# A conditioned two-layer decoder trunk: groups of three experts last in each layer, modulation loaded in pairs of vectors

## The chip, the cores and the metric

The kernel runs on one core of a Trainium2 chip. The metric is the device time in microseconds, median of the runs; lower is better. Engines are called as in the profile: PE is TensorE (PEld its weight loads), DVE is VectorE, ACT is ScalarE, POOL is GpSimd, SP is SyncE, which here only issues transfers.

## The reference, cut to what matters

One sequence of 256 rows of 1024 numbers (float32) goes through two layers and a final normalisation. `c` is a vector of 1024 that conditions every layer.

```python
for layer in range(2):
    shift_m, scale_m, gate_m, shift_f, scale_f, gate_f = split(silu(c) @ ada_w[layer] + ada_b[layer], 6)
    h = rmsnorm(x, norm_mix[layer]) * (1 + scale_m) + shift_m
    x = x + gate_m * (even_mixer if layer == 0 else odd_mixer)(h)
    h = rmsnorm(x, norm_ffn[layer]) * (1 + scale_f) + shift_f
    x = x + gate_f * grouped_moe(h)          # 16 experts, two per token
return rmsnorm(x, final_norm)
```

`ada_w[layer]` is 1024 x 6144 (25 MB), so the six modulation vectors of a layer cost 12 pieces of 2 MB. An expert has three matrices of 1024 x 512 (gate, up) and 512 x 1024 (down), 2 MB each; all 16 are read in both layers (201 MB of the 291 MB in all). The even mixer is sparse and block attention with a position bias, the odd one latent and sliding-window attention.

## The kernel before, in words

**Slots.** All weights go through a ring of tiles of 1 MB (128 partitions x 2048 float32): 10 of the pool `ring` (tag "w", `slot` in the trace) and 5 of the pool `rooms` (tag "wx", `room`). `slot()` takes the next one in the order that the list `order` gives; `left()` sets that order ahead of an MoE so that all 15 are used in turn. In the mixers the rooms hold attention data (`carve`). A load waits until the products that read the slot before are done. SP issues nearly all loads in program order.

**Modulation.** `fills` lists the pieces of 512 columns still to do, as (layer, n). `ada_load` loads one in two transfers (rows of 512 columns, 2 KB packets); `ada_chunk` multiplies it by silu(c): eight products of 32 x 512 (L332), four of them side by side in the four column groups of the array. The first half of a vector is copied out (L342), the second added (L344), and `ada_end` brings the vector into its place: eight small products for shift and scale (L307 to L313), or two products and two adds into the broadcast `GATE` (L301, L303). Four pieces are done at the start, ten within the even mixer by `ada_steps` (a piece every 9 ticks and a few more, between the mixer's own instructions), two at the MoE's start (`fill(12)`, with lowered priority); in layer 1 two at the start, four within, two at the MoE's start. ADC holds ada_b by feature, NRM the norms' gains.

**Bias rows.** `bias_line` writes the position bias of 8 heads to `scr` in DRAM; `bias_rows` (L407) reads it back by POOL's queue as 128 shifted rows, 1 MB.

**Experts.** `moe` routes each token to two experts. Experts 14 and 15 make the first group, whose weights need no routing. The other 14 are sorted by their count of tokens; `RANKS` gives the rank for each place, and `GROUPS` the places of each group with the number of blocks of 32 rows that each gets. Every group has four blocks (128 rows), so one tile of TensorE's output holds a group. Per group: `gather` (L1066), gate and up products (`hidden`, L1084, tiles `mm` and `sc`), a transpose, down products (`rows`, L1084, tile `o`) and `combine` (L1144, L1145). The loop runs gate and up of group i, then the down products of group i-1. Within a weight the slots come half by half, all experts of the group side by side.

**Overflow.** Ahead of group 3 stands `rest()`: nested branches (L1453) for tokens that found no place, on PE, ACT, DVE and SP. It allocates six slots. Group 2's down weights are loaded ahead of it, group 3's weights by POOL's queue:

```python
            if i == 3:
                before.load_down()
                flush()
                rest()
```

**The end.** In layer 1 the last group's down weights come in three column pieces (512, 256 and 256), with the final normalisation behind each (`Final`, `finish`).

Of the kernel before, what the change touches and what calls it, by code (L numbers as in the profile page):

```python
# [107 lines left out]
def trunk(ctx, tc, ins, out):  # L108
# [141 lines left out]
    def ada_load(layer, n):  # L250
        return load_k8(ins["ada_w"][layer][:, n * 512:(n + 1) * 512])

    first = [ada_load(0, n) for n in range(2)]
# [8 lines left out]
    first += [ada_load(0, n) for n in range(2, 4)]  # L262
    csil = cp.tile([P, 8, 33], F32, name="csil")
    vec.memset(csil, 0.0)
    act.activation(csil[:, :, 1], cT, AF.Silu)

    HALF = cp.tile([P, 2], F32, name="HALF")
    vec.tensor_reduce(HALF, ident.rearrange("p (g r) -> p r g", r=32)[:, 0:2], AX.X, ALU.add)
# [26 lines left out]
    def ada_end(layer, v, t):  # L295


        if v in (2, 5):
            for half in range(2):
                b = bank("tp", [P, 512])  # L300
                mm(b, HALF[:, half:half + 1].to_broadcast([P, P]), t, start=True, stop=True)  # L301
                sl = slice(half * 512, half * 512 + 512)
                vec.tensor_tensor(GATE[v][:, sl], GATE[v][:, sl], b, ALU.add)  # L303
            return
        b = bank("tp", [64, 8, 2])
        for k in range(8):
            mm(b[:, k, :], t[:, 64 * k:64 * k + 64], HALF, start=True, stop=True)  # L307
        o = MOD[layer, v]
        for half in range(2):
            sl = slice(64 * half, 64 * half + 64)  # L310
            vec.tensor_tensor(o[sl], b[:, :, half], ADC[sl, layer, v, :], ALU.add)
        if v in (1, 4):
            vec.scalar_tensor_tensor(o, o, 1.0, NRM[:, (v // 3) * 2 + layer, :], ALU.add, ALU.mult)  # L313
# [4 lines left out]
    fills = []  # L318

    halves = []  # L320

    def ada_chunk(layer, c, W):


        v, half = divmod(c, 2)
        if half == 0 and v in (2, 5):
            GATE[v] = big.tile([P, D], F32, name="GATE", tag="GATE")
            pool.dma_start(GATE[v], ins["ada_b"][layer:layer + 1, v * D:(v + 1) * D].to_broadcast([P, D]))
        b = bank("tp", [P, 512])
        for k in range(8):  # L330
            g = (k % 4) * 32
            mm(b[g:g + 32], csil[:, k, 1 - half:33 - half], W[k], start=k < 4, stop=k >= 4)  # L332
            if k == 3:
                yield
        if half == 0:
            halves.append(ada_tile())
        t = halves[0]
        o, i = t, b
        if v not in (2, 5):
            o, i = t.rearrange("p (k m) -> p m k", k=8), b.rearrange("p (m k) -> p m k", k=8)  # L340
        if half == 0:
            act.copy(o, i)  # L342
            return
        vec.tensor_tensor(o, o, i, ALU.add)  # L344
        yield
        ada_end(layer, v, halves.pop())

    def fill(n=1):
        for _ in range(n):
            if fills:  # L350
                layer, c = fills.pop(0)
                W = first.pop(0) if first else ada_load(layer, c)
                for _ in ada_chunk(layer, c, W):
                    pass

    def ada_steps(n, rest):
# [4 lines left out]
        for i, at in enumerate(todo):  # L361
# [3 lines left out]
            yield from ada_chunk(*at, W)  # L365
# [37 lines left out]
    def bias_rows(pool_):  # L403
# [3 lines left out]
        pool.dma_start(BM, bass.AP(scr.tensor, 0, [[1, P], [384, 8], [1, 256]]))  # L407
# [1370 lines left out]
```

## Time and profile before

| | |
|---|---|
| median of 3 runs | 868.94 us (868.36 to 869.42) |
| the profiled execution | 869.42 us, span 867.2 us |
| busy: PE, PEld, DVE, ACT, POOL | 746.6, 381.9, 377.8, 237.4, 115.6 us |
| mean granted TensorE clock | 0.932 of 2.4 GHz |
| transfers | 291.14 MB, mean 336 GB/s |

The span is from the first to the last instruction of the profiled execution. Layer 0's mixer runs to about 205 us, its router to 232, its experts to 472, layer 1's mixer to 596, its router to 618, its experts and the end to 867.

### The profile page before, as it was taken

What the parts mean: (1) busy time and instruction counts of PE and PEld (TensorE: products, weight loads), DVE (VectorE), ACT (ScalarE), POOL (GpSimd) and SP (SyncE); (2) the same over time, 40 slices, a digit from 0 to 9 for tenths busy, and PEclk for the clock granted to TensorE, in tenths of its full rate; (3) what the DMA queues carried; (4) which work ended last, traced back from release to release, by engine and by line L of the source; (5) the groups of instructions that cost most, each with busy time, mean ns of one, the idle gap of its engine ahead of it and who ended that gap; (6) DMA issues with size and microseconds to landing.
All of it is one profiled execution on the core that took longest, in us unless ns stands there. A gap on an engine that the chain in (4) does not pass through costs nothing. (4 is left out here: it accounts for less than half of the span.)

```text
span 867.2 us, 12251 instructions
## 1 busy us (share of the span) xinstructions
PE 746.6 (86%) x4499; PEld 381.9 (44%) x4499; DVE 377.8 (44%) x1091; ACT 237.4 (27%) x569; POOL 115.6 (13%) x118
## 2 busy tenths in 40 slices
PE   4699999999799969759997899979899967769996
PEld 1298765557443332214332568556443322214233
DVE  2285777767831231103206654876912031103214
ACT  1254545545311010001112454545111010002012
POOL 2020111233100001000011223344000001000001
PEclk9699999999699999879999999988699988979998
DMA  9999878796299998999999997733499989999992
GB/s 328 349 328 387 321 248 217 280 376 219 96 422 418 419 417 337 419 420 419 419 415 389 360 350 196 288 130 122 179 419 419 419 361 395 420 420 419 416 396 77
DMA packets 84840, 291.14 MB, mean 336 GB/s; under 512 B 9174, under 2 KB 23202, under 8 KB 63010
## 3 DMA queue, kind: packets, MB, share of 16 engines
q1 hardware_dynamic: 76976, 258.36, 77.9%
q0 software_dynamic: 4608, 29.37, 8.3%
q10 hardware_dynamic: 3186, 2.51, 0.9%
q8 instruction: 39, 0.64, 0.3%
q14 instruction: 31, 0.25, 0.1%
HBM read 289.16 MB, written 1.06 MB: 335 GB/s over the span
## 5 line engine op out<-in xcount | busy, mean ns | idle before, releaser
L1084 PE MATMUL o<-slot,hT 128*32 128x512 f32 (+2 forms) x448 | 93.5, 619 | 14.0 <-PEq L1453 13.1
L1084 PE MATMUL sc<-slot,XG 128*64 128x512 f32 (+1 forms) x416 | 92.1, 646 | 13.6 <-DMA slot<-in_moe_w_up_dram 13.6
L1111 DVE TENSOR_TENSOR hq<-sc,hid 128x512 f32<-128x512 f32 x14 | 14.7, 1049 | 184.3 <-PE sc L1084 184.3
L1084 PE MATMUL mm<-slot,XG 128*32 128x512 f32 (+1 forms) x416 | 85.9, 624 | 5.2 <-DMA slot<-in_moe_w_gate_dram 5.2
L507 ACT CAST hl<-slot 128x512 fp32r<-128x512 f32 (+2 forms) x112 | 60.7, 557 | 72.8 <-PE mm L524 45.8
L464 POOL TENSOR_TENSOR hl<-slot,hl 128x512 fp32r<-128x512 f32 x40 | 53.2, 1333 | 163.1 <-ACT hl L507 135.7
L1084 PE MATMUL mm<-room,XG 128*64 128x512 f32 (+1 forms) x224 | 57.1, 629 | 5.6 <-DMA room<-in_moe_w_gate_dram 5.6
L1084 PE MATMUL o<-room,hT 128*32 128x512 f32 (+2 forms) x208 | 58.6, 603 | 2.0 <-DMA room<-in_moe_w_down_dram 2.0
L1155 DVE SCALAR_TENSOR_TENSOR adac<-o,w,GATE 128x512 f32<-128x512 f32 (+1 forms) x29 | 21.2, 732 | 82.5 <-PE o L1084 81.5
L522 PE MATMUL mm<-HH,hl 128*128 128x256 f32 x176 | 54.5, 311 | 2.3 <-ACT HH L496 2.3
L1084 PEld LDWEIGHTS sc<-slot,XG 128*64 128x64 f32 (+1 forms) x416 | 25.3, 132 | 70.1 <-issue 48.6
L1137 ACT CAST yg<-adac 128x512 fp32r<-128x512 f32 (+1 forms) x28 | 17.1, 612 | 140.0 <-DVE adac L1155 140.0
L332 PE MATMUL tp<-slot,csil 128*32 128x512 f32 x344 | 49.2, 648 | 4.4 <-DMA slot<-in_ada_w_dram 4.2
L1084 PE MATMUL sc<-room,XG 128*32 128x512 f32 (+1 forms) x224 | 45.0, 656 | 8.3 <-DMA room<-in_moe_w_up_dram 8.3
L1068 ACT ACTIVATE XG<-tp,mod,mod 128x256 f32<-128x256 f32 (+1 forms) x32 | 17.2, 538 | 124.0 <-PE tp L1066 124.0
L524 PE MATMUL mm<-HH,hl 128*128 128x256 f32 x176 | 50.0, 286 | 0.6 <-DVE hl L464 0.6
L523 PE MATMUL mm<-HH,hl 128*128 128x256 f32 x176 | 50.4, 287 | 0.1
L1084 PEld LDWEIGHTS o<-slot,hT 128*32 128x32 f32 (+1 forms) x448 | 25.5, 125 | 54.3 <-issue 36.0
L464 DVE TENSOR_TENSOR hl<-slot,hl 128x512 fp32r<-128x512 f32 (+2 forms) x72 | 42.6, 611 | 15.3 <-ACT hl L507 15.0
L1066 PE MATMUL tp<-pick,XH 128*128 128x256 f32 (+1 forms) x128 | 41.9, 347 | 4.0 <-DVE XG L1070 2.6
L1145 DVE TENSOR_TENSOR X<-X,tp 128x512 f32<-128x512 f32 (+1 forms) x56 | 36.0, 675 | 16.5 <-PE tp L1144 16.2
L1144 PE MATMUL tp<-yg,OT 128*128 128x512 f32 (+1 forms) x112 | 36.6, 431 | 7.5 <-ACT yg L1137 3.5
(377 smaller groups left out, 1305.9 us busy)
## 6 DMA issues: line engine op xcount, KB each, us to landing
slot<-in_ada_w_dram SPq DMA_DIRECT2D x43, 1024.0 KB, 10.3
slot<-in_moe_w_gate_dram SPq DMA_DIRECT2D x37, 1024.0 KB, 15.1
slot<-in_moe_w_down_dram SPq DMA_DIRECT2D x35, 1024.0 KB, 19.7
slot<-in_moe_w_up_dram SPq DMA_DIRECT2D x34, 1024.0 KB, 18.6
room<-in_moe_w_up_dram SPq DMA_DIRECT2D x20, 1024.0 KB, 16.8
room<-in_moe_w_gate_dram SPq DMA_DIRECT2D x19, 1024.0 KB, 15.2
room<-in_moe_w_down_dram SPq DMA_DIRECT2D x17, 1024.0 KB, 18.8
slot<-in_ev_w_in_dram SPq DMA_DIRECT2D x8, 1024.0 KB, 9.5
```

The costliest lines, as they stand in the source:

```text
L332: mm(b[g:g + 32], csil[:, k, 1 - half:33 - half], W[k], start=k < 4, stop=k >= 4)
L464: eng.tensor_tensor(lo, v, hi.bitcast(F32), ALU.subtract)
L507: act.copy(hi, src)
L522: mm(o, a[0], b[0], start=start, stop=False, skip_group_check=True)
L523: mm(o, a[0], b[1], start=False, stop=False, skip_group_check=True)
L524: mm(o, a[1], b[0], start=False, stop=stop, skip_group_check=True)
L1066: mm(b, xk[i][:, t, k, :], o[:, t, 0:n], start=t == i == 0, stop=t == i == 1)
L1068: act.activation(XG[:, k, :], b, AF.Identity, bias=sh[:, k:k + 1], scale=fa[:, k:k + 1])
L1084: last[0] = mm(*args, **kw)
L1144: mm(cb, OT[:, t, :], x, start=i == 0, stop=i == 1)
L1145: vec.tensor_tensor(X[:, t, sl], X[:, t, sl], cb, ALU.add)
L1155: vec.scalar_tensor_tensor(v, y, w, gate[:, sl], ALU.mult, ALU.mult)
```

## The change

- **Order of groups.** Before, groups 2 and 4 have three experts; after, groups 5 and 6, the last two. The blocks that each rank gets are the same.
- **Modulation by two vectors at a time.** The vectors are paired as (0, 1), (2, 5) and (3, 4). `ada_load` loads 256 rows of both vectors (a part, (layer, n, j)), two transfers of 1 MB, each with 8 KB per partition (for the gates, 2 and 5, twice 4 KB). `ada_part` multiplies a part with eight products and adds four parts up (one copy, three adds). The small transposing products serve both vectors of a pair at once. Nothing of this is left at the MoE's start but `second_gate`, which spreads the sums of vector 5 (`GT5`) into `GATE`.
- **Steps.** `ada_steps` takes 12 parts in the even mixer, 6 in the odd one, each with 7 ticks of rest.
- **Bias rows.** In layer 0 the read of `scr` is issued after the last subtraction of `modulated`.
- The last group's down pieces are laid out for three experts.

```diff
-GROUPS = [[(14, 2), (15, 2)], [(0, 3), (1, 1)], [(2, 2), (3, 1), (4, 1)], [(5, 2), (6, 2)], [(7, 2), (8, 1), (9, 1)],
-          [(10, 2), (11, 2)], [(12, 2), (13, 2)]]
-RANKS = 0, 9, 1, 10, 11, 2, 3, 4, 12, 13, 5, 6, 7, 8
+GROUPS = [[(14, 2), (15, 2)], [(0, 3), (1, 1)], [(2, 2), (3, 2)], [(4, 2), (5, 2)], [(6, 2), (7, 2)],
+          [(8, 2), (9, 1), (10, 1)], [(11, 2), (12, 1), (13, 1)]]
+RANKS = 0, 9, 1, 2, 3, 4, 5, 6, 7, 10, 11, 8, 12, 13
...
-    def ada_load(layer, n):
-        return load_k8(ins["ada_w"][layer][:, n * 512:(n + 1) * 512])
+    TWOS = [(0, 1), (2, 5), (3, 4)]
+
+    def ada_load(layer, n, j):
+        v = ins["ada_w"][layer].rearrange("(p k) f -> p k f", k=8)
+        a, b = (x * D for x in TWOS[n])
+        out = []
+        for k in range(2 * j, 2 * j + 2):
+            t = slot(4, 512)
+            if b == a + D:
+                sp.dma_start(t.rearrange("p a b -> p (a b)"), v[:, k, a:a + 2 * D])
+            else:
+                sp.dma_start(t.rearrange("p (v a) b -> p v (a b)", v=2),
+                             v[:, k, :].rearrange("p (v f) -> p v f", f=D)[:, TWOS[n][0]::TWOS[n][1] - TWOS[n][0], :])
+            out.append(t)
+        return out
...
+    def second_gate(layer):
+        gate_start(layer, 5)
+        gate_end(5, 2, GT5)
...
+    def ada_part(layer, n, j, W):
+        gates = 2 in TWOS[n]
+        if j == 0:
+            if gates:
+                gate_start(layer, 2)
+            sums.append(GT5 if gates else ada_tile())
+        t = sums[0]
         b = bank("tp", [P, 512])
+        for k in range(2):
+            for g in range(4):
+                mm(b[32 * g:32 * g + 32], csil[:, 2 * j + k, :], W[k][:, g, :], start=k == 0, stop=k == 1)
...
+        if j == 0:
             act.copy(o, i)
+        else:
+            vec.tensor_tensor(o, o, i, ALU.add)
+        if j == 3:
+            yield
+            ada_end(layer, n, sums.pop())
...
-    def bias_rows(pool_):
+    def bias_rows(pool_, after=None):
         BM, = carve((8, 256))
-        pool.dma_start(BM, bass.AP(scr.tensor, 0, [[1, P], [384, 8], [1, 256]]))
+        with tc.issue_after(after.ins) if after else nullcontext():
+            pool.dma_start(BM, bass.AP(scr.tensor, 0, [[1, P], [384, 8], [1, 256]]))
...
         with tc.high_priority(-60):
-            fill(12)
+            second_gate(layer)
...
-            ada.add(ada_steps(10, 9))
+            ada.add(ada_steps(12, 7))
...
-    ada.add(ada_steps(4, 9))
+    ada.add(ada_steps(6, 7))
```

## Rows read from the trace of the kernel before

**Rows 1.** The page, rate of all transfers in 40 equal slices of the span.

```profile
GB/s 328 349 328 387 321 248 217 280 376 219 96 422 418 419 417 337 419 420 419 419 415 389 360 350 196 288 130 122 179 419 419 419 361 395 420 420 419 416 396 77
```

**Rows 2.** Chosen stretches: us, busy PE, PEld, DVE, ACT, POOL, clock, DMA share, GB/s.

```profile
45.00:205.00 160.00, 157.43 (x1108) 111.75 (x1108) 116.43 (x382) 84.55 (x230) 32.75 (x26) 1.00 0.88 303
326.50:331.50 5.00, 5.00 (x40) 1.49 (x36) 0.00 (x0) 0.00 (x0) 1.59 (x3) 0.74 0.33 87
618.00:704.00 86.00, 81.42 (x544) 34.39 (x543) 28.78 (x89) 12.74 (x24) 1.69 (x3) 0.95 1.00 412
618.00:712.50 94.50, 83.71 (x556) 35.06 (x559) 30.23 (x92) 12.74 (x24) 1.69 (x3) 0.93 1.00 410
712.50:717.00 4.50, 4.50 (x36) 1.34 (x32) 0.00 (x0) 0.00 (x0) 1.44 (x3) 0.75 0.31 76
717.00:836.00 119.00, 98.45 (x532) 33.55 (x524) 22.44 (x40) 12.39 (x22) 3.34 (x7) 0.93 1.01 418
836.00:847.00 11.00, 9.66 (x43) 3.27 (x43) 3.38 (x5) 1.82 (x4) 0.00 (x0) 1.00 1.05 363
847.00:867.20 20.20, 12.51 (x67) 6.19 (x66) 9.69 (x21) 5.92 (x18) 3.89 (x4) 0.86 0.16 60
```

**Rows 3.** Timeline of SP's queue and of POOL at layer 1's branch.

```profile
686.77 0.33 SPq L1171 DMA_DIRECT2D room<-in_moe_w_down_dram  x1
715.19 1.30 SPq L1171 DMA_DIRECT2D room<-in_moe_w_gate_dram  x2
...
690.70 0.62 POOL L1171 DMA_DIRECT2D slot<-in_moe_w_gate_dram  x1 [82.67 <-PE o L1084]
...
697.41 0.53 POOL L1171 DMA_DIRECT2D room<-in_moe_w_gate_dram  x1 [0.20 <-issue]
715.09 0.53 POOL L1171 DMA_DIRECT2D room<-in_moe_w_gate_dram  x1 [17.14 <-SPq L1453]
```

**Rows 4.** Timeline of PE: group 2's gate (second half), group 1's down, after the branch.

```profile
675.33 3.62 PE L1084 MATMUL mm<-slot,XG 128*32 128x512 f32 x32
...
686.70 3.64 PE L1084 MATMUL o<-slot,hT 128*32 128x512 f32 x32 [0.88 <-DMA slot<-in_moe_w_down_dram]
...
710.22 1.06 PE L1084 MATMUL o<-slot,hT 128*32 128x512 f32 x2 [6.23 <-PEq L1453]
```

**Rows 5.** Timeline of DVE at the end: the last group's last piece.

```profile
857.84 0.48 DVE L1155 SCALAR_TENSOR_TENSOR adac<-o,w,GATE 128x256 f32<-128x256 f32 x1 [0.51 <-PE o L1084]
```

**Rows 6.** Timeline of PE, DVE and POOL at the start, up to the modulated rows.

```profile
34.47 1.94 PE L332 MATMUL tp<-slot,csil 128*32 128x512 f32 x8 [0.72 <-DMA slot<-in_ada_w_dram]
...
29.34 0.33 DVE L311 TENSOR_TENSOR mod<-tp,ADC 64x8 f32<-64x8 f32 x2 [3.92 <-DMA ADC<-in_ada_b_dram]
...
39.51 0.33 DVE L311 TENSOR_TENSOR mod<-tp,ADC 64x8 f32<-64x8 f32 x2 [1.96 <-PE tp L307]
...
46.61 2.90 POOL L464 TENSOR_TENSOR HH<-hv,HH 128x512 fp32r<-128x512 f32 x1 [2.29 <-ACT HH L496]
```

**Rows 7.** Transfers issued in the first 30 us: size, us to landing.

```profile
room<-scr POOLq DMA_DIRECT2D x1, 1024.0 KB, 11.1
...
ADC<-in_ada_b_dram ACTq DMA_DIRECT2D x1, 48.0 KB, 22.8
```

**Rows 8.** The softmax's line that reads the bias rows: ns, first and last start.

```profile
L569 DVE CUSTOM_DVE_ANT_0 St<-sc,room x72: 277/354/426, 92.5 to 574.7; 128x128 f32<-128x128 f32 x36, 128x256 f32<-128x256 f32 x36
```

**Rows 9.** Modulation's lines L332 (two stretches), L307 and L303, busy us there.

```profile
45.00:205.00 160.00, 20.48 (x160) 4.20 (x160) 1.00 0.88 303
484.00:596.00 112.00, 8.11 (x64) 1.46 (x64) 0.94 0.73 256
...
45.00:205.00 160.00, 4.32 (x64) 4.03 (x64) 1.00 0.88 303
...
472.00:484.00 12.00, 1.37 (x2) 1.00 1.09 335
```

**Rows 10.** Timeline of DVE in layer 0's router, behind the position sums.

```profile
226.61 0.19 DVE L1042 SCALAR_TENSOR_TENSOR route<-sc,M 128x32 f32<-128x32 f32 x1 [0.85 <-PE sc L1360]
```

More of the change, by code (lines that the diff above doesn't have):

```diff
@@ L248, in trunk @@
     act.dma_start(OH, ins["k_onehot"])
-    def ada_load(layer, n):
-        return load_k8(ins["ada_w"][layer][:, n * 512:(n + 1) * 512])
-    first = [ada_load(0, n) for n in range(2)]
+    TWOS = [(0, 1), (2, 5), (3, 4)]
[12 more added lines that the diff above has]
+        return out
+    first = [ada_load(0, 0, j) for j in range(4)]
     load_const(0, cp)
@@ L261, in trunk @@
     act.dma_start(ADC.rearrange("p l v k -> p (l v) k"), ins["ada_b"].rearrange("l (v p k) -> p (l v) k", p=P, k=8))
-    first += [ada_load(0, n) for n in range(2, 4)]
-    csil = cp.tile([P, 8, 33], F32, name="csil")
+    csil = cp.tile([P, 8, 32], F32, name="csil")
     vec.memset(csil, 0.0)
-    act.activation(csil[:, :, 1], cT, AF.Silu)
-    HALF = cp.tile([P, 2], F32, name="HALF")
-    vec.tensor_reduce(HALF, ident.rearrange("p (g r) -> p r g", r=32)[:, 0:2], AX.X, ALU.add)
+    act.activation(csil[:, :, 0], cT, AF.Silu)
     ONES = cp.tile([P, P], F32, name="ONES")
@@ L293, in trunk, with gate_end, gate_start, ada_end @@
     GATE = {}
-    def ada_end(layer, v, t):
-        if v in (2, 5):
-            for half in range(2):
[L300 to L313, printed above, removed]
+    def gate_end(v, g, t):
+        for half in range(2):
+            b = bank("tp", [P, 512])
+            r = 32 * (g + half)
+            mm(b, ident[:, r:r + 1].to_broadcast([P, P]), t, start=True, stop=True)
+            sl = slice(half * 512, half * 512 + 512)
+            vec.tensor_tensor(GATE[v][:, sl], GATE[v][:, sl], b, ALU.add)
+    def gate_start(layer, v):
+        GATE[v] = big.tile([P, D], F32, name="GATE", tag="GATE")
+        pool.dma_start(GATE[v], ins["ada_b"][layer:layer + 1, v * D:(v + 1) * D].to_broadcast([P, D]))
+    def second_gate(layer):
+        gate_start(layer, 5)
+        gate_end(5, 2, GT5)
+    def ada_end(layer, n, t):
+        if 2 in TWOS[n]:
+            gate_end(2, 0, t)
+            return
+        b = bank("tp", [64, 8, 4])
+        for k in range(8):
+            mm(b[:, k, :], t[:, 64 * k:64 * k + 64], ident[:, 0:128:32], start=True, stop=True)
+        for i, v in enumerate(TWOS[n]):
+            o = MOD[layer, v]
+            for half in range(2):
+                sl = slice(64 * half, 64 * half + 64)
+                vec.tensor_tensor(o[sl], b[:, :, 2 * i + half], ADC[sl, layer, v, :], ALU.add)
+            if i:
+                vec.scalar_tensor_tensor(o, o, 1.0, NRM[:, (v // 3) * 2 + layer, :], ALU.add, ALU.mult)
     def ada_tile():
@@ L318, in trunk @@
     fills = []
[L320 to L328, printed above, removed]
+    GT5 = cp.tile([P, 512], F32, name="GT5")
+    sums = []
+    def ada_part(layer, n, j, W):
[5 more added lines that the diff above has]
+        t = sums[0]
         b = bank("tp", [P, 512])
[L330 to L333, printed above, removed]
+        for k in range(2):
+            for g in range(4):
+                mm(b[32 * g:32 * g + 32], csil[:, 2 * j + k, :], W[k][:, g, :], start=k == 0, stop=k == 1)
+            if k == 0:
                 yield
-        if half == 0:
-            halves.append(ada_tile())
-        t = halves[0]
         o, i = t, b
-        if v not in (2, 5):
+        if not gates:
             o, i = t.rearrange("p (k m) -> p m k", k=8), b.rearrange("p (m k) -> p m k", k=8)
-        if half == 0:
+        if j == 0:
             act.copy(o, i)
[L343 to L346, printed above, removed]
+        else:
[3 more added lines that the diff above has]
+            ada_end(layer, n, sums.pop())
     def fill(n=1):
@@ L350, in fill @@
             if fills:
-                layer, c = fills.pop(0)
-                W = first.pop(0) if first else ada_load(layer, c)
-                for _ in ada_chunk(layer, c, W):
+                at = fills.pop(0)
+                W = first.pop(0) if first else ada_load(*at)
+                for _ in ada_part(*at, W):
                     pass
@@ L1261, in load_down @@
                     n = sl.stop - sl.start
-                    if n == 512:
-                        tiles = [slot(4, n) for _ in range(2)]
-                    else:
-                        tile_ = slot(8, n)
-                        tiles = [tile_[:, 0:4], tile_[:, 4:8]]
+                    tiles = []
+                    while len(tiles) < len(src):
+                        tile_ = slot(2048 // n, n)
+                        tiles += [tile_[:, j:j + 4] for j in range(0, 2048 // n, 4)]
                     for k in range(0, 4, step):
```

20 lines of the change are left out of this document (9 added, 11 removed).

## The prediction

> **What bounds the kernel now.** I read the page's slices first, for the rate of the transfers along the run [rows 1]. The slices show three kinds of stretch: the first five at 321 to 387 GB/s, the two mixture-of-experts (MoE) stages at about 420, and the ends of the two mixers far below. The reader is to see that a transfer saved is worth something only in the first and second kind.
>
> The busy times of chosen stretches say which engine goes with it [rows 2]. From 45 to 205 us TensorE is busy 157.4 of 160 us while the transfers run at 303 GB/s: the even mixer is bound by TensorE. In layer 1's MoE the transfers run at 410 to 418 GB/s from 618 to 836 us with one gap, 712.5 to 717, and a slower end, 836 to 847 (363 GB/s). Then 20.2 us follow in which nothing is loaded. Layer 0 has the same gap, 326.5 to 331.5. So an MoE stage costs its 96 tiles of 1.05 MB (2.5 us each at 418 GB/s), plus the gap, plus what is left to compute after the last byte.
>
> The queues show where the gap comes from [rows 3]. At group 3 the overflow branch (L1453) stands in the program. SP issues its last tile of group 2 at 686.77 and its next at 715.19, so it is 28.4 us in the branch. GpSimd's queue carries group 3 meanwhile: three tiles by 697.41, the fourth only at 715.09, released by SP's leaving. TensorE stands 6.23 us in the branch and leaves at 710.22 [rows 4].
>
> **The order of groups, at the branch.** The ring has 15 slots (10 and 5), and `rest()` holds 6 of them. In the code's order the tiles after the first group are: gate, up of 1; down of 0; gate, up of 2; down of 1; down of 2; the 6 held; group 3. With three experts in group 2 that is 4+4+4+6+6+4+6 = 34, and 15 - 6 - 6 = 3 of group 3 find a slot before the branch is left: 37 tiles. 410 GB/s over 94.5 us is 38.7 MB, which is those 37 [rows 2]. With two experts in group 2 it is 28, and 15 - 6 - 4 = 5 of group 3: 33 tiles. The cover falls by four tiles, 10.0 us, so the queues run dry at 702.5.
>
> When do they start again? TensorE's work before the branch is the same: a group has four blocks of 32 rows either way, and TensorE is busy 81.4 of 86 us from 618 to 704 [rows 2], so it is the bound there; it loses only a wait of 0.88 us for a down tile that now comes sooner [rows 4]. It leaves at 709.3. SP's last tile waits for group 2's first gate tiles, consumed by 675.33 [rows 4]; 28.4 us later, at 703.9, SP is out, before TensorE. From the release to bytes flowing took 1.9 us (715.09 to 717). So bytes flow at 711.2: a gap of 8.7 us where it was 4.5, **+4.2 us in layer 1**. Layer 0 has the same sequence and a gap of 5.0: **+4.2** there too, since its last down tiles end the stage. Bounds for each: 0, if TensorE comes through the branch 4 us sooner; +9, if the first slot is freed only by group 2's down products after the branch, some 5 us later.
>
> **The order of groups, at the end.** Now the last group has two experts (30 us of transfers); TensorE follows the transfers by so much that it still works for 11 us after the last byte. With 45 us of transfers for the same TensorE work in each of the last two groups, TensorE waits for bytes. What is left after the last of them is half of the last 256-column piece and the chain that follows it: the last row scaling starts at 857.84 and the span ends at 867.2, 9.4 us [rows 5]; I add 2.0 for the products of the last half piece and the wait for their landing, which is 11.4 in place of 20.2: **-8.8**. Bounds: 0 (TensorE at 1.2 GHz falls behind again) and -10. The last group's down weights come in pieces of 1 and 2 KB packets; one expert more is 2.1 MB at 363 instead of 418 GB/s [rows 2]: **+0.8**.
>
> **Modulation at the start.** The last weights of scale and shift land at 34.47, and the vectors are ready from 39.51 on; a wait for the bias vectors ADC ends at 29.34 [rows 6]. Eight loads of 1.05 MB are 8.39 MB. In the fourth slice, where packets of 2 KB go, the rate is 387 GB/s [rows 1]; 8 KB packets go at 418 in the MoE [rows 2]: 1.7 us less. The bias rows' 1 MB, 11.1 us under way here [rows 7], leaves this stretch: 2.7 us less at 387 GB/s. It is covered later: the last modulated piece ends at 49.51 [rows 6], and the bias rows' first reader in the softmax starts at 92.5 [rows 8]. Together 4.4 us, if ADC keeps its time. ADC is 48 KB and needed 22.8 us [rows 7], among neighbours of 2 KB. With neighbours of 8 KB it can come later; at the worst it eats the whole gain. I take **-3.5**, bounds -6 (a lighter queue lets X and ADC come sooner too) and 0.
>
> The Trainium skill (DMA: Bandwidth & Descriptors, Specifications) gives 512 B as the least transfer for line rate. By it the larger packets would bring nothing and the sum below would be 1.7 us higher. The slices disagree, 387 against 418, and I go by them.
>
> **Modulation in the mixers.** A unit of 2 MB costs TensorE 20.48 / 10 = 2.05 us in the even mixer and 8.11 / 4 in the odd one; the four transposing ends between 45 and 205 us cost 4.32 [rows 9]. Two units per layer move from the MoE's start into the mixer, since both gates are now summed together. Even mixer: +4.1 for two units, and two ends instead of four, -2.2: **+1.9** on the engine that binds it. Bounds 0 and +5 (four adds more on VectorE, 1 us each). Odd mixer: +4.1 and one end less, -1.1, make 3.0, of which half falls in idle time of TensorE (I have no row that says which half; bounds 0 and 3.0): +1.5. The gate's two adds leave the stretch just ahead of it, 1.37 us of VectorE [rows 9]: -1.4. Sum **+0.1**.
>
> The 4 MB per layer that leave the MoE's start bring no transfer time: the queues stand nearly idle there (96 GB/s in the eleventh slice) [rows 1], as the experts aren't known yet. What goes is work among the router's: in layer 0 VectorE waits 0.85 us for a product that stands behind the gate's [rows 10]: **-0.9** (bounds 0 and -3 over both layers). The gate's bias load, two broadcasts and adds stay; their data is ready sooner.
>
> **Sum.** Start -3.5, even mixer +1.9, router -0.9, layer 0's gap +4.2, odd mixer +0.1, layer 1's gap +4.2, small packets +0.8, tail -8.8: -2.0. The profiled execution took 869.42 us (span 867.2 and 2.2 around it), so 867.4; the median of the runs is 0.5 lower, so **866.9 us**.
>
> **Rivals.** *A later restart (slower).* The first slots after the branch come with group 2's down products, not with TensorE's leaving. Place: GpSimd's sixth tile of group 3. Price 5 us in each layer: 876.9. It decides from 1 us later per layer on. For it: a ring slot is reused in turn. Against: in the trace the fourth tile was released by SP's leaving [rows 3]. Chance 0.12.
>
> *The tail stays (slower).* TensorE, idle between arrivals, drops to 1.2 GHz and comes as late as before: +8.8, 875.7. For it: the mean clock is 0.93 from 717 to 836, where one group of three experts lies [rows 2]. Against: even there it kept pace. Chance 0.10.
>
> *ADC late (no change).* The gain at the start goes: 870.4. For it: ADC's 22.8 us [rows 7]. Chance 0.20. The Trainium skill (DMA: Bandwidth & Descriptors, Queues, rings and completion order) says that an engine goes round its queues packet by packet, which would make longer neighbours delay such a load; no row shows this with 8 KB neighbours.
>
> *The gap doesn't grow (faster).* TensorE or the walk through the branch is earlier by as much as the cover is shorter: -8.4, 858.5. Against: TensorE's 81.4 of 86 us. Chance 0.13.
>
> **Numbers.** My forecast has the remaining 0.45, with its own range of 863 to 871. Some 0.2% (1.7 us) is about what a measurement here can tell from no change. Faster: 0.6 of the forecast, the last rival, a little of ADC's: 0.44. Slower: the first two rivals, a tenth of the forecast and a quarter of ADC's: 0.31. Same: 0.25. The range reaches from the last rival to the tail that stays: 858 to 876.
>
> **What would show it.** Right: transfers dry for 8 to 9 us after the first 33 tiles in each layer, SP back before TensorE; 11 to 12 us from the last byte to the end; vectors of scale ready at about 36; TensorE as full as before from 42 to 205. Wrong: a gap of under 5 or over 13 us, a tail near 20, or ADC as the last wait ahead of the scale.

## The result and the profile after

The changed kernel takes **872.67 us** (median of 8 runs, 871.32 to 876.65), the kernel before, run beside it, 867.6 (8 runs): ratio **1.0065**, 95% interval 1.0047 to 1.0083. It is slower by 5 us; the forecast was 866.9, 2.0 under the median of before as then known. The profiled execution took 871.63 us, with a span of 870.0 (before 867.2).

I put marks at the same instructions of both traces: the even mixer's first projection (L522 before, L548 after), the first transposing product of layer 0's router (L982, L1008), the product that counts the routed tokens (tile M), layer 0's last down product, the count in layer 1, and the end. The stages between them:

| stage | before, us | after, us | difference | forecast |
|---|---|---|---|---|
| start | 41.77 | 36.56 | -5.2 | -3.5 |
| even mixer | 167.60 | 174.13 | +6.5 | +1.9 |
| router of layer 0 | 16.93 | 16.48 | -0.5 | -0.9 |
| experts of layer 0 | 241.10 | 243.90 | +2.8 | +4.2 |
| odd mixer, router of layer 1 | 145.09 | 144.99 | -0.1 | +0.1 |
| experts of layer 1 and the end | 254.71 | 253.94 | -0.8 | -3.8 (+4.2 +0.8 -8.8) |
| span | 867.20 | 870.00 | +2.8 | -2.0 |

Two stages miss: the even mixer by 4.6 us, the last one by 3.0. The start was better than forecast. The stages are those of one execution of each kernel. The medians stand 5.1 us apart because the traced execution of before lies 1.8 above its median and that of after 1.0 below (2.2 + 1.8 + 1.0); what varies between executions, e15 shows.

**The start.** PE, DVE and POOL, as in [rows 6]:

```profile
28.61 1.06 PE L359 MATMUL tp<-slot,csil 128*32 128x512 f32 x8 [1.48 <-DMA slot<-in_ada_w_dram]
30.81 1.87 PE L331 MATMUL tp<-K,adac 128*64 128x4 f32 x16 [1.14 <-DVE adac L368]
36.56 0.80 PE L548 MATMUL mm<-HH,hl 128*128 128x256 f32 x2 [3.88 <-ACT HH L522]
...
32.72 0.68 DVE L336 TENSOR_TENSOR mod<-tp,ADC 64x8 f32<-64x8 f32 x4 [1.96 <-PE tp L331]
...
44.10 0.96 POOL L433 DMA_DIRECT2D room<-scr  x1
```

The last weights land 5.9 us sooner than in [rows 6] and the vectors are there at 32.72 in place of 39.51. The prediction had them ready at about 36. The add that reads ADC waits for TensorE: ADC is not the last wait. The transfers run faster there; two stretches of before, then the same of after:

```profile
10.00:20.00 10.00, 5.29 (x22) 2.63 (x15) 4.27 (x9) 2.82 (x6) 2.59 (x3) 1.00 1.07 371
20.00:30.00 10.00, 7.32 (x60) 2.88 (x58) 1.33 (x3) 1.07 (x1) 0.00 (x0) 0.93 1.07 356
```

```profile
10.00:20.00 10.00, 6.70 (x30) 3.03 (x26) 4.39 (x10) 2.82 (x6) 1.09 (x2) 0.85 1.02 396
20.00:30.00 10.00, 6.60 (x54) 1.31 (x46) 2.37 (x3) 1.06 (x1) 0.00 (x0) 0.98 1.03 392
```

**The even mixer**, as stretches in the columns of [rows 2], first the whole mixer of the kernel before, then of the one after:

```profile
41.77:209.37 167.60, 164.97 (x1136) 118.02 (x1137) 122.55 (x393) 90.07 (x240) 34.22 (x27) 0.99 0.88 305
```

```profile
36.56:210.69 174.13, 168.10 (x1137) 116.77 (x1137) 127.67 (x396) 87.37 (x237) 35.23 (x28) 0.99 0.84 306
...
195.00:200.00 5.00, 2.64 (x12) 1.54 (x12) 5.00 (x9) 2.92 (x6) 3.60 (x3) 1.00 0.01 2
200.00:210.00 10.00, 9.85 (x46) 7.21 (x46) 7.21 (x13) 4.72 (x9) 1.29 (x1) 1.00 0.01 2
```

TensorE has 3.1 us more work and 3.4 us more idle time (6.0 against 2.6). The largest piece of the idle time is a hole of 2.4 us from 195 to 200, where VectorE is full. PE's longest waits in the changed kernel's mixer:

```profile
107.33 0.65 PE L650 MATMUL o<-PT,room 128*64 128x256 f32 x4 [1.53 <-DVE PT L225]
...
197.56 0.63 PE L643 MATMUL tp<-K,St 128*128 128x128 f32 x4 [0.89 <-DVE St L633]
199.76 0.49 PE L549 MATMUL mm<-hl,o 128*128 128x512 f32 x1 [1.33 <-DVE hl L490]
```

VectorE ends each of them. In the kernel before, no wait within the mixer is over 0.71 us.

**The branches.** Stretches of layer 0 and layer 1, then SP, POOL and PE in layer 1, as in [rows 2 to 4]:

```profile
304.00:324.50 20.50, 14.35 (x87) 6.49 (x81) 8.12 (x19) 3.88 (x7) 3.47 (x7) 0.91 0.69 255
690.00:712.50 22.50, 16.20 (x104) 7.34 (x106) 8.42 (x20) 3.88 (x7) 2.82 (x6) 0.94 0.76 283
```

```profile
711.29 10.23 SPq L1197 DMA_DIRECT2D slot<-in_moe_w_gate_dram  x4
...
687.68 0.62 POOL L1197 DMA_DIRECT2D slot<-in_moe_w_gate_dram  x1 [76.56 <-DMA slot<-in_moe_w_down_dram]
694.81 1.21 POOL L1197 DMA_DIRECT2D slot<-in_moe_w_gate_dram  x2 [6.52 <-PE o L1110]
701.47 0.53 POOL L1197 DMA_DIRECT2D room<-in_moe_w_gate_dram  x1 [5.45 <-PE o L1110]
702.15 0.53 POOL L1197 DMA_DIRECT2D room<-in_moe_w_up_dram  x1 [0.15 <-issue]
711.56 0.53 POOL L1197 DMA_DIRECT2D room<-in_moe_w_up_dram  x1 [8.88 <-PEq L1478]
...
711.47 1.09 PE L1110 MATMUL o<-slot,hT 128*64 128x512 f32 x1 [4.02 <-PEq L1478]
```

Against a steady 419 GB/s the first stretch loses 20.5 x (1 - 255/419) = 8.0 us, the second 7.3. The same sum for the two stretches of [rows 2] gives 4.0 and 3.7. So each branch costs 3.6 to 4.0 us more, as forecast. The form is another than forecast: the queues run short from 304 and from 694 on, and live on slots that TensorE's down products free one by one. The count of slots held: five tiles of group 3 are issued ahead of TensorE's leaving, which releases the sixth at 711.56. SP's next load had by then waited 13.1 us for TensorE, so SP was back first, as forecast.

**The end.** Stretches, PE and DVE in the last 24 us, as in [rows 2, 5]:

```profile
846.00:854.00 8.00, 6.11 (x35) 2.18 (x36) 3.79 (x6) 0.62 (x1) 0.00 (x0) 1.00 1.07 341
854.00:856.00 2.00, 2.00 (x30) 1.09 (x34) 1.28 (x2) 0.89 (x3) 0.68 (x1) 1.00 0.31 95
```

```profile
849.63 1.92 PE L1110 MATMUL o<-slot,hT 128*32 128x512 f32 x16
853.13 1.46 PE L1170 MATMUL tp<-yg,OT 128*128 128x512 f32 x4 [1.58 <-ACT yg L1163]
854.52 1.93 PE L1110 MATMUL o<-room,hT 128*32 128x256 f32 x32
...
858.61 1.07 PE L1110 MATMUL o<-slot,hT 128*32 128x256 f32 x16
...
860.64 0.48 DVE L1181 SCALAR_TENSOR_TENSOR adac<-o,w,GATE 128x256 f32<-128x256 f32 x1
```

The stretch from 854 to 856 carries 0.19 MB, which is half a microsecond at 341 GB/s: the last byte lands at about 854.5, 15.5 us before the end. From the last row scaling to the end it is 9.4 us, the forecast's figure to the tenth. From the last byte to that scaling it is 6.1 us where 2.0 were forecast. The rows show why: TensorE stands still from 851.5 to 853.13 for the first piece's rows, since their combining product is queued ahead of the second piece's products.

### The profile page after: what moved, and what is told of

The parts are those of the page before. It is cut to its first block, busy times and chain, and to the rows that moved or that the text cites. A ratio compares the mean times of both kernels' runs of the same rounds, so it can differ in the third digit from the quotient of the medians.

```text
span 870.0 us, 12146 instructions
## 1 busy us (share of the span) xinstructions
PE 743.3 (85%) x4451; PEld 380.1 (44%) x4451; DVE 383.3 (44%) x1100; ACT 231.3 (27%) x563; POOL 112.5 (13%) x118
## 3 DMA queue, kind: packets, MB, share of 16 engines
HBM read 289.16 MB, written 1.06 MB: 334 GB/s over the span
## 5 line engine op out<-in xcount | busy, mean ns | idle before, releaser
L1110 PE MATMUL sc<-slot,XG 128*32 128x512 f32 (+1 forms) x464 | 91.1, 610 | 14.1 <-DMA slot<-in_moe_w_up_dram 14.1
L1110 PE MATMUL o<-slot,hT 128*32 128x512 f32 (+2 forms) x384 | 84.5, 618 | 14.9 <-PEq L1478 8.2
L490 POOL TENSOR_TENSOR hl<-slot,hl 128x512 fp32r<-128x512 f32 x40 | 52.8, 1325 | 176.8 <-ACT hl L533 159.1
L1110 PE MATMUL o<-room,hT 128*32 128x512 f32 (+2 forms) x288 | 66.3, 663 | 7.0 <-DMA room<-in_moe_w_down_dram 7.0
L548 PE MATMUL mm<-HH,hl 128*128 128x256 f32 x176 | 54.6, 311 | 3.9 <-ACT HH L522 3.9
L1110 PEld LDWEIGHTS sc<-slot,XG 128*32 128x32 f32 (+1 forms) x464 | 25.7, 123 | 68.0 <-issue 46.7
L359 PE MATMUL tp<-slot,csil 128*32 128x512 f32 x384 | 51.0, 617 | 3.7 <-DMA slot<-in_ada_w_dram 3.5
L490 DVE TENSOR_TENSOR hl<-slot,hl 128x512 fp32r<-128x512 f32 (+2 forms) x72 | 45.6, 655 | 16.9 <-ACT hl L533 16.0
L1110 PE MATMUL mm<-room,XG 128*32 128x512 f32 (+1 forms) x192 | 50.5, 637 | 1.5 <-DMA room<-in_moe_w_gate_dram 1.5
L1110 PEld LDWEIGHTS o<-slot,hT 128*32 128x32 f32 (+1 forms) x384 | 23.1, 128 | 59.2 <-issue 41.5
L1110 PE MATMUL sc<-room,XG 128*32 128x512 f32 (+1 forms) x176 | 47.0, 615 | 0.0
```

The source lines that it names most:

```text
L359: mm(b[32 * g:32 * g + 32], csil[:, 2 * j + k, :], W[k][:, g, :], start=k == 0, stop=k == 1)
L490: return eng.tensor_tensor(lo, v, hi.bitcast(F32), ALU.subtract)
L548: mm(o, a[0], b[0], start=start, stop=False, skip_group_check=True)
L1110: last[0] = mm(*args, **kw)
```

## The experiments

Ratios are against the kernel before on the same chip, with their 95% interval.

**e1: the order of groups alone.** The kernel before with `GROUPS`, `RANKS` and the tiles of the last down pieces for three experts, as in the change.

> The kernel before with only the new order of groups (and the last down pieces laid out for three experts); modulation and bias rows as before. Stage account read from the two traces: layer 0's branch +3.7 us, layer 1's branch and small packets +5.3, the end -5.2, so +3.8 on the kernel before, about 871.4 us. The account of the prediction (+4.2, +4.2, +0.8, -8.8) gives +0.4, about 868.0. If the loss in the branches came with the modulation's change of the slots' order instead, this kernel would be 5 us faster than before, about 862.5.

Measured: 874.95 us, ratio 1.0078 (1.0057 to 1.0098), 6 us slower and above all three expectations. Its trace has the experts of layer 0 at 248.1 us, 7.0 more than before, and those of layer 1 with the end at 254.35. Its last down products in layer 0, and those of the changed kernel (timeline of PE):

```profile
469.02 1.06 PE L1084 MATMUL o<-room,hT 128*32 128x512 f32 x1 [5.89 <-DMA room<-in_moe_w_down_dram]
```

```profile
468.02 0.62 PE L1110 MATMUL o<-slot,hT 128*32 128x512 f32 x2 [2.15 <-DMA slot<-in_moe_w_down_dram]
```

After a wait of 5.9 us the same product takes 1.06 us (granted clock 0.64 from 465 to 470), after 2.15 us it takes 0.62 (1.00 from 465 to 471.7): the lower clock, for five such steps, costs e1 another 2 us there. The order of groups alone loses as much as the whole change. How much of that falls to layer 0 is uncertain, since the changed kernel itself has 243.9 us there in one execution and 247.3 in another (e15).

**e2: the modulation and bias rows alone.** The changed kernel with the old `GROUPS` and `RANKS`.

> The changed kernel with the old order of groups, so modulation by two vectors and the late bias rows alone. Stage account read from the two traces: start -5.2, even mixer +6.5, router -1.3, odd mixer +0.3, second router -1.3, so -1.0, about 866.6 us. The account of the prediction (-3.5, +1.9, -0.9, +0.1) gives -2.4, about 865.2. In the trace the first projection stays near 36.6 us and layer 0's router starts near 210.7.

Measured: 869.55 us, ratio 1.0011 (0.9996 to 1.0027), above both expectations and no clear change. First projection at 36.17, router at 210.85: the start's gain is there and the even mixer takes it back, whatever the groups are.

**e3: three-expert groups at places 2 and 6.**

```diff
-GROUPS = [..., [(2, 2), (3, 2)], [(4, 2), (5, 2)], [(6, 2), (7, 2)],
-          [(8, 2), (9, 1), (10, 1)], [(11, 2), (12, 1), (13, 1)]]
+GROUPS = [..., [(2, 2), (3, 1), (4, 1)], [(5, 2), (6, 2)], [(7, 2), (8, 2)],
+          [(9, 2), (10, 2)], [(11, 2), (12, 1), (13, 1)]]
```

> The changed kernel with the three-expert groups at places 2 and 6 (before: 2 and 4; after: 5 and 6). If the cover of 37 tiles at the branch is what was lost, both dry stretches go back to about 4.5 us, 8 us less in all; if one group of 45 us of transfers at the end is enough for TensorE to catch up with the transfers, the tail stays at about 15 us: together about 864.5 us. Rival: the short tail needs both last groups, the tail goes back to 20 us: about 869.8. Rival: the dry stretch comes from something else than the order and stays: about 872.7.

Measured: 865.7 us, ratio 0.9969 (0.9953 to 0.9985). Stretches at the branch of layer 1, and the last bytes:

```profile
700.00:710.00 10.00, 3.81 (x19) 1.19 (x22) 2.28 (x6) 0.00 (x0) 0.00 (x0) 0.75 0.94 383
710.00:720.00 10.00, 10.00 (x68) 2.61 (x60) 1.44 (x2) 0.62 (x1) 2.64 (x5) 0.91 0.70 270
...
845.00:846.00 1.00, 0.56 (x2) 0.30 (x2) 0.58 (x1) 0.39 (x1) 0.00 (x0) 1.00 0.30 97
```

The dry stretch costs 0.9 + 3.6 = 4.4 us again, what it cost before, so the cover of 37 tiles is what was lost. And one group of three experts at the end does for the tail: the last byte lands at about 845.1, 16.7 us before the end of the span (861.8).

**e4: adds on GpSimd.** In the even mixer:

```diff
-            vec.tensor_tensor(o, o, i, ALU.add)
+            act.copy(c, b)
+            pool.tensor_tensor(o, o, c, ALU.add)
```

> The changed kernel with the modulation's adds within the even mixer taken from VectorE (nine of 0.93 us) and done by a copy on ScalarE and an add on GpSimd. If VectorE's added work is what makes TensorE idle in the even mixer (3.4 us more idle than before), the router of layer 0 starts about 3.4 us sooner (207.3 in place of 210.7) and the run takes about 869.3 us. If the idle time comes from where the parts stand in TensorE's order, it stays within 1 us of the changed kernel, 872.7. If GpSimd's longer add delays the next part or VectorE beside it, it is slower than 873.5.

Measured: 877.59 us, ratio 1.0099 (1.0080 to 1.0118). The router starts at 217.70. VectorE has 7.3 us less to do in the mixer, which takes 7.0 us longer: the third case, a slower add in the chain. TensorE waits three times for GpSimd's adds, 2.4 us in all; a part of the rest is the lower clock (0.83 from 200 to 210, 1.00 in the changed kernel).

**e5: four adds fewer.**

```diff
-        else:
+        elif j == 3 or (layer, n, j) < (0, 1, 0) or layer:
             vec.tensor_tensor(o, o, i, ALU.add)
```

> The changed kernel with four of the nine adds of the even mixer's modulation left out (the second and third part of the gates and of shift and scale for the experts of layer 0 are multiplied but not added), so VectorE has five adds there, as many as before. If the four more adds, 0.93 us each, are what the even mixer lost, layer 0's router starts 3.4 to 3.7 us sooner than at 210.7 and the run takes about 869.2 us. If the loss is in where the parts stand in TensorE's order, the router starts within 1 us of 210.7 and the run takes about 872.7.

Measured: the router at 211.34. VectorE's work is back at 122.8 us, as before, and the mixer takes 175.28. But the clock fell ahead of the router (0.88 from 200 to 210), as in e15, so this time does not compare with the changed kernel's. The time up to the product that ends the hole does better: 162.60 us from the first projection, against 163.20 in the changed kernel and 163.89 in e15. So four adds are worth 0.6 to 1.3 us, not 3.4, and the hole stays: my account that VectorE's adds cost the 3.4 us falls. One wait does go, that of 1.53 us at 107.33. DVE and POOL just ahead of it in the changed kernel, then DVE in e5:

```profile
105.17 1.50 DVE L633 TENSOR_SCALAR St<-St,r 128x128 f32<-128x128 f32 x2
...
105.32 1.27 POOL L490 TENSOR_TENSOR hl<-slot,hl 128x512 fp32r<-128x512 f32 x1 [3.64 <-ACT hl L533]
```

```profile
104.73 0.48 DVE L633 TENSOR_SCALAR St<-St,r 128x128 f32<-128x128 f32 x2
```

In the changed kernel VectorE's row scalings run beside an instruction of GpSimd and take 1.50 us. In e5, with an add less ahead of them, they end before GpSimd starts (105.39) and take 0.48. (The kernel leaves four adds out, so tokens go elsewhere, and layer 1's branch is walked through with work in it: 903.39 us.)

**e6: 6 ticks of rest.** `ada_steps(12, 6)`.

> The changed kernel with 6 in place of 7 ticks of rest between the parts in the even mixer, so the last of them comes some 12 ticks, about 12 us, sooner. If the idle 2.4 us of TensorE from 195 to 200 us come from the last part standing ahead of the last softmax rows, they go: the router at about 208.3 and the run at about 870.3 us. If VectorE's adds are the cause, nothing changes (872.7). If earlier parts push the attention back as much, nothing changes either, with the idle time elsewhere.

Measured: 870.46 us, ratio 1.0038 (1.0017 to 1.0058). The router starts at 209.80, less early than expected. The hole is nearly gone (columns of [rows 2]) and TensorE's idle time falls from 6.0 to 4.2 us; but its busy time is 1.5 us longer (169.59 against 168.10), so the mixer gains only 0.3:

```profile
35.98:209.80 173.82, 169.59 (x1136) 117.34 (x1137) 123.68 (x397) 88.30 (x237) 34.21 (x28) 0.98 0.86 307
...
195.00:200.00 5.00, 4.55 (x25) 3.20 (x27) 4.50 (x9) 2.92 (x8) 4.02 (x3) 1.00 0.18 74
```

**e7: three-expert groups at places 1 and 6.**

```diff
-GROUPS = [[(14, 2), (15, 2)], [(0, 3), (1, 1)], [(2, 2), (3, 2)], ...
+GROUPS = [[(14, 2), (15, 2)], [(0, 2), (1, 1), (2, 1)], [(3, 3), (4, 1)], ...
```

> The changed kernel with the three-expert groups at places 1 and 6. By the count of slots 39 tiles are on their way before the branch is left, in place of 37 with places 2 and 6 and 33 in the changed kernel. If the cover alone decides, each dry stretch shrinks by two tiles (5 us) to nothing, and the run takes 857 to 861 us, against 865.7 with places 2 and 6. Rival: SP's way through the branch (28.4 us after its last tile) moves back as well, since its last tile comes later, and the dry stretch stays: 865.7. Rival: TensorE waits for the first groups' bytes, which come 5 us later: 865 to 870.

Measured: 860.75 us, ratio 0.9921 (0.9894 to 0.9948). The same two stretches of layer 1 as in e3:

```profile
700.00:710.00 10.00, 5.51 (x32) 1.75 (x24) 5.27 (x8) 1.62 (x3) 1.59 (x3) 0.99 1.02 422
710.00:720.00 10.00, 6.57 (x44) 1.96 (x48) 0.90 (x4) 0.00 (x0) 1.59 (x3) 0.66 0.98 385
```

They lose 0.8 us in place of 4.4. The count of slots, which forecast the loss, finds the gain as well.

**e8: the end in order,** on e3. `combine` gets the chain of the products (`put`), and one chain runs through all pieces:

```diff
+                put = in_line()
                 for i, sl in enumerate(end.pieces):
                     y = bank("o", [P, sl.stop - sl.start])
-                    put = in_line()
...
-                            combine(self.OT, rows, sl)
+                            combine(self.OT, rows, sl, put)
```

> Places 2 and 6, and in the last group TensorE's products of the second and third column piece are put ahead of the combining products of the piece before. In the run with places 2 and 6 the last row scaling starts 7.9 us after the last bytes (845.1 to 852.96), since TensorE first waits for the first piece's rows. If that order is what makes the end longer than the forecast 11.4 us, the last row scaling comes some 3 us sooner: about 862.7 us, 13 to 14 us from the last byte to the end. Rival: VectorE and ScalarE, which bring the pieces' rows, set the end: 865 to 866.

Measured: 861.83 us, ratio 0.9923 (0.9895 to 0.9951). PE and DVE at the end:

```profile
843.17 1.92 PE L1110 MATMUL o<-slot,hT 128*32 128x512 f32 x16
844.92 1.91 PE L1110 MATMUL o<-room,hT 128*32 128x256 f32 x32
...
850.30 0.48 DVE L1181 SCALAR_TENSOR_TENSOR adac<-o,w,GATE 128x256 f32<-128x256 f32 x1 [0.74 <-PE o L1110]
```

The second piece follows the first without a wait. From the last byte (846.4) to the last row scaling it is 3.9 us in place of 7.9 in e3, and 13.5 to the end of the span (859.9) in place of 16.7. So the order of TensorE's queue is the larger part of what kept the tail from the forecast 11.4: 3.2 of 5.3 us. The other 2.1 are open.

**e9: places 1 and 6, end in order, 6 ticks.** The edits of e7, e8 and e6 together.

> The changed kernel with the three-expert groups at places 1 and 6, the end in order as in the run before, and 6 ticks of rest. If the three gains add up (places 1 and 6: 860.75; the end -3.9 as between the two runs with places 2 and 6; rest 6: -2.2), about 854.7 us. If the end's order and the cover at the branch overlap, 857 to 860.

Measured: 856.90 us, ratio 0.9885 (0.9867 to 0.9903): 15.8 us under the changed kernel, where the three gains add up to 18.0 (runs on different chips).

**e10: bias rows early.** `bias_rows(cp)` in place of `bias_rows(cp, done)`.

> The changed kernel with the bias rows' transfer issued where the kernel before has it. The prediction gave 2.7 us of the start to the deferral: the first projection then comes 2 to 3 us later (at about 39 in place of 36.6). If the even mixer is bound from its first product on, the run is 2 to 3 us longer, about 875.3. If the mixer gives back what the start gains, whatever it is, the router of layer 0 stays at 210.7 and the run at 872.7.

Measured: 874.98 us, ratio 1.0091 (1.0069 to 1.0113). First projection at 39.91, router at 215.62. The deferral is worth 3.3 us of the start (forecast 2.7). The other 1.9 are left to the new modulation; the forecast gave 1.7 to the larger packets, and from 10 to 20 and 20 to 30 us the transfers do run at 402 and 398 GB/s here, with the bias rows among them in the second, where the kernel before had 371 and 356. And the mixer does not give back whatever the start gains: up to the product that ends the hole it takes 163.28 us, as long as in the changed kernel (163.20). (The rest of the later router, 1.5 us, is a lower clock, 0.83 from 200 to 210.)

**e11: ten parts in the even mixer.**

```diff
-    fills += [(0, n, j) for n in range(3) for j in range(4)] + [(1, 0, j) for j in range(4)]
+    fills += [(0, n, j) for n in range(3) for j in range(4)] + [(1, 0, j) for j in range(2)]
...
-            ada.add(ada_steps(12, 7))
+            ada.add(ada_steps(10, 9))
```

> The changed kernel with ten parts in the even mixer, each after 9 ticks, as many units and as much rest as the kernel before has there: the last two parts of layer 1's first pair are left out (so layer 1's shift and scale for its mixer are sums over half of c, and its routing may differ: only the time up to layer 0's router counts). If the two more units are what the mixer lost, the router comes about 6 us sooner than at 210.7 (204 to 205). If they cost what was forecast (4.1 us of TensorE), it comes at about 206.5. If the loss has nothing to do with the amount of work, it stays near 210.7.

Measured: the router at 202.95, the mixer 166.86 us (kernel before 167.60):

```profile
36.09:202.95 166.86, 164.09 (x1104) 116.12 (x1105) 121.39 (x395) 88.08 (x237) 35.30 (x28) 0.98 0.84 295
```

Two parts fewer take 4.0 us of work and 3.3 us of idle time away: 3.6 us for each part, where the prediction gave 2.05. So its price was right for the work, and the idle time is what it left out. The rest between parts changed as well here (9 ticks for 7); e6 and e14 show that 6 and 8 ticks alone bring no more than 2.2 us.

**e12: the kernel before with places 1 and 6 and the end in order.**

> The kernel before, with its old modulation and bias rows, with the three-expert groups at places 1 and 6 and the end in order. If the modulation's change is worth nothing here (changed modulation alone measured 1.0011 of before), it is as fast as the same places and end with the new modulation, 857 to 859 us. If the new modulation's 1 us of the trace is real, 1 to 2 us slower than that.

Measured: 861.43 us, ratio 0.9937 (0.9917 to 0.9958), above both expectations. With the new modulation and 6 ticks (e9) the same order is 4.5 us faster. The 6 ticks were worth 2.2 (e6), so about 2 us are left for the new modulation. That is an estimate over several chips, and e2, where the new modulation alone gained nothing, speaks against it.

**e13: four parts at the router,** on e9: `ada_steps(8, 9)`, and behind the routing

```diff
             second_gate(layer)
+            if not layer:
+                spare[0] = lambda: wk.tile([P, 512], F32, tag="hid", name="hid", bufs=1)
+                fill(4)
+                spare[0] = None
```

> Places 1 and 6, the end in order, and the four parts of layer 1's first pair taken out of the even mixer (eight parts left there, 9 ticks of rest each) and put behind the routing at the start of layer 0's experts, where the queues carry next to nothing and TensorE waits 5.7 us. If a part costs the even mixer 3.6 us, as ten against twelve parts suggest, the router comes 12 to 14 us sooner (196 to 198 in place of 209.6) and the four parts cost 3 to 8 us behind it: about 848 to 852 us, against 856.9 with the parts in the mixer. If a part costs what TensorE's products of it take (2.05), the router comes 8 us sooner and the same 8 us come back at the start of the experts: about 857.

Measured: **847.07 us**, ratio **0.9762** (0.9737 to 0.9786), the fastest of all, 2.4% under the kernel before. The mixer, then the router:

```profile
35.96:197.28 161.32, 157.94 (x1057) 114.49 (x1057) 120.58 (x389) 86.70 (x236) 34.39 (x28) 0.98 0.85 302
197.28:214.69 17.41, 16.10 (x96) 8.83 (x95) 12.01 (x42) 9.22 (x11) 6.68 (x3) 0.80 0.77 299
```

The mixer is 11.9 us shorter than e9's 173.19, the router 1.0 longer and the experts of layer 0 2.8 longer. The four parts, with the transposing end that goes with them, cost the mixer 3.0 us each (9.3 us in all by the prediction's prices; the rest between parts changed too, from 6 to 9 ticks), and behind the router, where the queues were empty and TensorE waited, 3.8 us in all.

**e14: 8 ticks of rest.** `ada_steps(12, 8)`.

> The changed kernel with 8 ticks of rest between the twelve parts. If the pace of the parts makes TensorE's idle time (6.0 us in the mixer with 7 ticks, 4.2 with 6, 2.8 with ten parts and 9 ticks), it differs here as well, by a us or more either way, with the busy time as before (168 us). If it is the amount of work that makes it, the idle time stays between 4 and 6 us and the router near 210.

Measured: 872.66 us, ratio 1.0055 (1.0036 to 1.0074). In its trace the mixer takes 180.89 us with 8.0 us idle, but the clock fell ahead of the router there, as in e15, so the numbers do not compare with the changed kernel's. By the median, the pace from 7 to 8 ticks does nothing.

**e15: the changed kernel once more.**

> The changed kernel itself once more, for a second profile. Its times fell into two groups, 871.3 to 873.1 and 876.1 to 876.7. If layer 0's branch or the end of its experts makes the difference (2.8 us over before in the trace at hand, 7.0 in the run with the groups alone), a profile of the upper group shows that stage 3 to 5 us longer and all others the same. If the even mixer varies, it shows there.

Measured: 872.68 us, ratio 1.0053 (1.0033 to 1.0072), runs from 870.97 to 877.05. This profile is of an execution of 877.05 us:

```profile
195.00:200.00 5.00, 3.40 (x20) 1.94 (x19) 5.00 (x10) 3.68 (x10) 4.53 (x4) 1.00 0.00 2
200.00:210.00 10.00, 9.12 (x30) 6.26 (x31) 4.87 (x10) 2.27 (x4) 1.29 (x1) 0.66 0.00 1
```

In the first profile the stretch from 200 to 210 had a granted clock of 1.00; here it is 0.66, part of it at 1.2 GHz, behind the same hole in TensorE's work. The mixer takes 3.5 us longer, the experts of layer 0 3.4 longer, the odd mixer 2.1 less. So the hole costs more than its 2.4 us in some executions. The clock fell behind it in the traces of e5 and e10 too, not in those of e2, e3, e7, e8 and e16. The experts of layer 0 end here as in e1: a wait of 3.94 us for down weights, then products of 1.07 us. The Trainium skill (TensorE: Matmul & The Clock Gate, What's actually happening) says that the number of products at the lower clock at a kernel's start differs between runs of one kernel; a fall in mid-run, as here, is not in that passage.

**e16: the first output projection's adds off GpSimd,** in the even mixer.

```diff
-            side.add(out_proj(OT, 0, wA, (vec, pool)))
+            side.add(out_proj(OT, 0, wA, (vec, vec)))
```

> The changed kernel with the four adds of the even mixer's first output projection (1.3 us each on GpSimd) moved to VectorE (about 0.7 each). In the changed kernel's trace VectorE's last row scalings take 0.77 us each where GpSimd adds beside them, and TensorE has a hole at 195 to 200 us. If these stalls make the hole, it goes (TensorE over 4 of 5 us busy there, the mixer 2 to 4 us shorter), the clock no longer falls ahead of the router in any run, and the median drops to 869 to 870.5 us. If VectorE's added 2.8 us cost as much as the stalls, it stays at 872.7; if VectorE is what binds there, it is slower.

Measured: 871.67 us, ratio 1.0041 (1.0024 to 1.0059), none of 11 runs above 873.55. DVE and POOL in the changed kernel, then the same instruction and the next pair in e16, with its stretches:

```profile
194.51 1.54 DVE L633 TENSOR_SCALAR St<-St,r 128x128 f32<-128x128 f32 x2
...
193.34 2.63 POOL L730 TENSOR_TENSOR X<-X,tmp 128x512 f32<-128x512 f32 x2
```

```profile
194.81 0.47 DVE L633 TENSOR_SCALAR St<-St,r 128x128 f32<-128x128 f32 x2
196.30 1.68 DVE L633 TENSOR_SCALAR St<-St,r 128x256 f32<-128x256 f32 x2
...
195.00:200.00 5.00, 3.59 (x25) 1.99 (x21) 4.99 (x11) 2.99 (x7) 2.63 (x2) 1.00 0.00 2
200.00:210.00 10.00, 9.23 (x40) 6.96 (x39) 8.16 (x15) 4.67 (x9) 1.29 (x1) 1.00 0.01 2
```

Beside GpSimd's adds the two row scalings take 1.54 us, without them 0.47. The Trainium skill (SBUF — State Buffer, SBUF: two separate sides) says that GpSimd and a VectorE instruction in a two-port mode lock one port pair against each other, each for its whole instruction. The longer scalings agree; the profile does not show the mode. But of the hole a part only moves behind 200: from 195 to 210 TensorE idles 2.2 us in place of 2.5, and the mixer is 0.3 shorter. The adds were not all that ran beside VectorE: the next pair of scalings, 0.61 us without GpSimd (at 185.36), still takes 1.68 beside another GpSimd instruction (L490), and that one was not moved in any run.

**e17: the same on e13.**

> Places 1 and 6, the end in order, four parts behind the router (847.07 us), and the same four adds on VectorE. If the stalls beside GpSimd cost something there too, 845 to 846.5 us; if the hole came from the late parts and is gone with them, 847 within 1 us.

Measured: 848.75 us, ratio 0.9763 (0.9735 to 0.9791): no change against e13.

## Why the prediction was wrong

Two steps failed, the even mixer by 4.6 us and the tail by 4.1; neither alone makes up the 5.1 us by which the median is longer. Of whole kernels, the order of groups alone measured 6.0 us slower where its terms gave +0.4 (e1), and the modulation and bias rows alone no clear change, 1.0011, where theirs gave -2.4 us (e2).

*The even mixer* is the first: "+1.9 on the engine that binds it", bounds 0 and +5, measured +6.5. Its count was right: the products of two units more and two ends fewer (24.54 + 2.19 us against 20.48 + 4.32) make 1.9. But a unit was priced at TensorE's busy time, as if that engine alone bound the stretch, and TensorE's waits were put at nothing in the sum (only its upper bound allowed for VectorE's adds). They grew by 3.4 us: TensorE was to be as full as before, and was busy for 96.5% of the mixer in place of 98.4. Ten against twelve parts (e11) and eight against twelve (e13) give 3.0 to 3.6 us for each, with the rest between parts changed too. VectorE ends the longest of the waits, but four adds are worth only 0.6 to 1.3 us (e5). At 107 us and in the hole, VectorE's row scalings run beside an instruction of GpSimd and take 1.5 us where they take 0.5 alone; the first of these waits goes when they do not meet (e5), and the hole nearly closes with a tick less (e6). That such meetings make all of the hole is argued from the rows, not shown: e16 took away only some of them. About 1 us of busy time in excess of the products stays open. All of the start's gain was spent in the mixer.

*The tail* is the second, mis-sized: -8.8 forecast. The mechanism was right, since TensorE caught up with the transfers. "2.0 for the products of the last half piece and the wait for their landing" measured 6.1, for the larger part because a combining product that waits stands ahead of products whose weights are there (e8). That leaves -4.7 for the tail.

*The gap* was right in size: +4.2 for each branch, measured 3.6 to 4.0 by the stretches of the transfers, and e3 and e7 confirm the count of tiles both ways. The restart came as forecast, with TensorE's leaving. (675.33 + 28.4 is 703.7, not 703.9; nothing hangs on it.) Its form was wrong: not a single dry stretch of 8 to 9 us, but a rate that breaks down ahead of the branch.

*The start* was right in sign and too small: -3.5 forecast, -5.2 measured; e10 splits it into 3.3 for the bias rows and 1.9 for the rest, which the prediction gave to the packets. (8.39 MB at 387 and at 418 GB/s differ by 1.6 us, not 1.7.) The Trainium skill's rule on the least transfer (DMA: Bandwidth & Descriptors, Specifications) would have made the packets' part nothing; the rates of e10, 402 and 398 GB/s against 371 and 356, speak against it.

*The router and the odd mixer* came within 0.4 us of their terms; the parts of those sums were not read one by one, so this may be luck.

*The rivals.* ADC was not late. The gap did grow. The restart was not later: TensorE's leaving released it. The tail neither stayed nor went as far as forecast. That TensorE drops to 1.2 GHz between arrivals shows in layer 0's end (e1, granted clock 0.64), where it cost 2 us. None of the rivals had the mixer, so the chance for slower, 0.31, was too low for a reason that none of them named.

## What to carry to other kernels

Work moved into a stretch that an engine fills can cost more than that engine's busy time, as it did here, since it also shifts the waits between the engines; the price is had by taking a few units out, not from the mean duration of one. Look for the place where queues and engine both wait: the same four parts and their end cost 12 us in the mixer and 3.8 behind the router. And when the order of transfers is changed, count which slots are free at the stall itself: two three-expert groups could serve two ends, one early for the cover and one last for the tail.

## What was not expected of the hardware

The same program ran 3.5 us longer in its even mixer when the granted clock was 0.66 in place of 1.00 from 200 to 210 us, behind the same hole of TensorE (e15). A row scaling of VectorE took 0.77 us beside GpSimd's adds and 0.24 without them (e16), 0.75 and 0.24 beside and ahead of another GpSimd instruction (e5). A product took 1.06 us after a wait of 5.9 us, 1.07 after one of 3.94, 0.62 after one of 2.15 (e1, e15 and the changed kernel).
